# A hybrid mixer layer: the small attention products of two chunks merged into one step, and some weight and key steps moved

## The chip, the cores and the metric

The kernel runs on one core of a Trainium2 chip. The metric is device time in microseconds (us) for one execution. TensorE is called PE in the profile, VectorE DVE, ScalarE ACT, GpSimd POOL, and SyncE, which issues DMAs, SP.

## The reference, cut to what matters

1024 prompt tokens and 64 sample tokens (8 sequences of 8) pass one layer with 1024 channels. One input projection feeds two mixers and their gates:

```
u, gp, q, k, v, gg, fa = split(x @ w_in)          # 512, 512, 256, 256, 512, 512, 16 columns
# pooling: per group of 128 channels a trailing mean over 2/4/8/16 tokens, minus the token, then a 128x128 map
pool_out = (mean_window(u) - u) @ w_map * scale
# gated linear attention, 4 heads, key width 64, value width 128, decays from fa
S_t = diag(a_t) S_{t-1} + k_t^T v_t ;  o_t = q_t S_t ;  o = o * rsqrt(mean(o*o) + eps) * norm_g
mix = concat(pool_out * silu(gp), o * silu(gg))
out = LayerNorm(alpha * x + mix @ w_out) * ln_g + ln_b
```

All of it is in 32-bit floats. The outputs are the tokens' results, the last pooling inputs, and the attention states of prompt and samples.

## The kernel before

**Split products.** Each large product takes its operands as a high and a low part of reduced precision (`split`: ScalarE copies the high part, VectorE or GpSimd subtracts the low one) and runs three matmuls (`mm3`, lines L68 to L70). Prompt attention runs in eight blocks of 128 tokens, c = 0 to 7 (`gla_steps(c)`), the samples are c = 8; the projection runs in three token chunks `CH` of 384, 384 and 320.

**Stages.** First come the value products (`psv`, to 58 us), with decay factors worked out beside them. Then sixteen rows of the projection, i = 0 to 15, each over the three chunks: `group(i, c)` is 24 matmuls into one `psm` tile. The rows are: 0 to 3 keys and queries, 4 to 7 the pooling input u, 8 to 11 the pooling gate, 12 to 15 the attention gate. The out product with `w_out` follows, from 291 us.

**What sets the order.** Small steps are put into a list by `later(delay, step)`. Behind each group, `tick()` runs the steps that have come due, in the order of their due numbers, and counts one slot on. In this text slot 0 is the group (4, 0), at 111.8 us. For a u group, VectorE's pool chain (`chain()`: window sums `ws`, difference `pd`, its split `pdhl`) is issued behind the tick, and its map product `psmap` later. When c is 0, the weights of row i+1 are split there: ScalarE the high part, GpSimd the low one (`hl` in the profile).

**The small steps of block c.** Line numbers are those of the profile before.

- s1, at number 2c: two PE transposes of the keys into the first 256 columns of a tile `pskt` (L712), four score products (L717), with keys and queries 64 deep, into the other half of `pskt` and into `psa`; then ScalarE copies the keys out (`kt`, L719) and VectorE masks the scores (`am`, L723).
- s2, at 2c+1: kt·v, four products of 64 columns of keys into the first half of `psp_` (L753); the inter products of state and queries, 64 deep (L761), and the intra products with `am` (L763), both into the second half of `psp_` and into `pso`; then the new state `S` by VectorE from `psp_` (L776, L777), squares by ScalarE (`sq`, L799) and their split `sqhl`.
- s3, at 2c+3: sums of squares (`psms`, L808); ScalarE loads a function table, takes Ln and Exp (L810 to L812); VectorE scales the block's output (`vm`, L818).

So an even slot 2c holds s1 of block c, an odd slot 2c+1 holds s3 of block c−1 and s2 of block c.

**The end of the projection.** Behind group (15, 1), `transition()` splits the first mix tile (`mx`) and the second slice of `w_out` (`split_w(17)`); behind group (15, 2) come its gate (silu on ScalarE, three products on VectorE, L401), the third slice, and the loads and splits of the other slices (`split_wo`). `sample_state_prep`, issued in the second round of the out loop, has GpSimd mask the samples' keys (L574) and decay their states. A `safe` variant of everything is built beside the fast one; it does not run with these inputs.

Of the kernel before, what the change touches and what calls it, by code (L numbers as in the profile page):

```python
# [15 lines left out]
D = 1024  # L16
# [23 lines left out]
class Body:  # L40
# [54 lines left out]
    def emit(self):  # L95
# [109 lines left out]

        def split_w(i):
            t = hlp.tile([128, 2, 8, 128] if i < 16 else [128, 2, 1024], F32, tag="hl", name="hl")
            self.split(t[:, 0], t[:, 1], raws.pop(("w", i)), on_lo=nc.gpsimd if i < 16 else None)
            wt[i] = t


# [111 lines left out]
        for t in range(3):  # L323
# [2 lines left out]
            (0, 1, 2): [("s", 2, 0), ("w", 1)],  # L326
            (1, 0, 0): [("lr",)],
            (1, 0, 1): [("s", 2, 4)],
            (2, 1, 0): [("sw", 0), ("w", 2)],
        }  # L330
        def low_rank_weight():

# [36 lines left out]
        def group(i, c):  # L369
            chain = None  # L370
            kind, m = order[i]
            o, n = CH[c]
            ps = psp.tile([128, 512], F32, tag="p", name="psm")
            for k in range(8):
                self.mm3(ps[:, :n], wt[i][:, 0, k], wt[i][:, 1, k], xt_hi[c][:, k], xt_lo[c][:, k], k == 0, k == 7)
            src = ps[:, :n]
            if kind == "k":
                if safe:
                    nc.vector.tensor_copy(self.K[:, m, o:o + n], src)
                else:  # L380
                    nc.vector.tensor_tensor(self.K[:, m, o:o + n], src, EK[:, m, o:o + n], op=ALU.mult)
            elif kind == "q":
                if safe:
                    nc.vector.tensor_scalar(self.Q[:, m, o:o + n], src, 0.125, None, op0=ALU.mult)
                else:
                    nc.vector.scalar_tensor_tensor(self.Q[:, m, o:o + n], src, 0.125, EQ[:, m, o:o + n],
                                                   op0=ALU.mult, op1=ALU.mult)
            elif kind == "u":
                chain = self.pool_steps(m, c, src)
            elif kind == "gp":  # L390
                sg = self.sgp.tile([128, 384], F32, tag="sg", name="sg")
                nc.scalar.activation(sg[:, :n], src, AF.Silu)
                pm = self.pmix[:, m, o:o + n]
                nc.vector.tensor_tensor(pm, pm, sg[:, :n], op=ALU.mult)
            else:
                sg = self.sgp.tile([128, 384], F32, tag="sg", name="sg")
                nc.scalar.activation(sg[:, :n], src, AF.Silu)  # L397
                for t in range(3 * c, 3 * c + 3):
                    _, to, tn = tiles[t]
                    pg = self.v[t][:, m, :tn]  # L400
                    nc.vector.scalar_tensor_tensor(pg, sg[:, to:to + tn], self.norm[:, m:m + 1], pg,  # L401
                                                   op0=ALU.mult, op1=ALU.mult)
            self.tick()
            if chain is not None:
                chain()
            if c == 0:
                split_w(i + 1)
                load_w(i + 3)
            if c == 1 and i == 15:
                self.transition()  # L410
# [13 lines left out]
        self.S = None  # L424
        for c in range(9):
            steps = self.gla_steps(c)
            at = [2 * c, 2 * c + 1, 2 * c + 3] if c < 8 else AT8
            for w, step in zip(at, steps):
                self.later(w, step)

# [2 lines left out]
        def load_wo(k):  # L433
            if k < 6:
                t = lnp.tile([128, D], F32, tag="hh", bufs=3, name="wr")
            else:
                t = rawp.tile([128, D], F32, tag="raw", name="wr")
            nc.sync.dma_start(t, io["w_out"][k])
            wraw[k] = t

# [21 lines left out]
        def transition():  # L462
            split_mix(0)
            split_w(17)

        self.transition = transition

        for i in range(4, 16):
# [13 lines left out]
            if i == 14:  # L482
                for k in (3, 4, 5):
                    load_wo(k)
        split_w(18)
        load_wo(6)
        for k in range(3):
            wo[k] = wt[16 + k]
        split_wo(3)
# [52 lines left out]

        split_wo(4)
        split_wo(5)
        load_wo(7)
        split_wo(6)
        split_wo(7)
        nc.scalar.preload_act_table_set(EXP_LN)
        for j, t in enumerate(OUT_ORDER):
            if j + 1 < 9:  # L550
                split_mix(OUT_ORDER[j + 1])
            out_tile(t)
            if j + 2 < 9:
                load_res(OUT_ORDER[j + 2])
            if j == 1:
                self.sample_state_prep()
            if j == 6:
                for q, pp in enumerate(self.sample_state_mm(0)):
                    self.sample_state_out(0, q, pp)()
# [5 lines left out]
            self.close(name)  # L565


    def sample_state_prep(self):
        nc = self.nc
        t = self.xp.tile([128, 2, 2048], F32, tag="xc2", name="s1")  # L570
        self.s1 = t[:, 0].rearrange("k (p b v) -> k p b v", p=2, b=NB)
        self.km = t[:NS, 1].rearrange("k (b c) -> k b c", b=NB)
        nc.sync.dma_start(self.s1, self.io["s0"])
        nc.gpsimd.tensor_tensor(self.km, self.kt8.unsqueeze(1).broadcast_to([NS, NB, 256]),  # L574
                                self.bmask.unsqueeze(2).broadcast_to([NS, NB, 256]), op=ALU.mult)
        for p in range(2):
            nc.gpsimd.tensor_tensor(self.s1[:, p], self.s1[:, p],
                                    self.dec[:, p, 8:16].unsqueeze(2).broadcast_to([128, NB, 128]), op=ALU.mult)

    def sample_state_mm(self, p, old=False):  # L580

# [92 lines left out]
    def gla_steps(self, c):  # L674
# [23 lines left out]
                st["kd"] = kd  # L698

        def s1():  # L700
            Kst, Qi = K, Q
            am = gl.tile([128, 4, 128], F32, tag="am", bufs=1, name="am")
            st["am"] = am
            if self.safe:
                Kst, Qi = self.safe_scores(c, am, t0, n, sample)
# [4 lines left out]
            pa = [pk[:, 256:], None]  # L710
            for p in range(2):
                nc.tensor.transpose(pk[:n, p * 128:(p + 1) * 128], Kst[:, p], self.ident)  # L712
            if not self.safe:
                pa[1] = g_tile("psa1")
                for h in range(4):
                    r, p = rows[h % 2], h // 2
                    nc.tensor.matmul(pa[h % 2][:n, p * n:(p + 1) * n], K[r, p], Q[r, p], start=True, stop=True)  # L717
            kt = self.kt8 if sample else gl.tile([128, 256], F32, tag="kt", bufs=1, name="kt")
            nc.scalar.activation(kt[:n], pk[:n, :256], AF.Copy)  # L719
            st["kt"] = kt  # L720
            if not self.safe:
                for e in range(2):
                    nc.vector.tensor_tensor(am[:n, two(e), :n], pa[e][:n, :2 * n].rearrange("s (p t) -> s p t", p=2),  # L723
                                            msk[:n, :n].unsqueeze(1).broadcast_to([n, 2, n]), op=ALU.mult)
# [9 lines left out]
        def sample_inter():  # L734
# [9 lines left out]
            st["in"] = gl.tile([128, 512], F32, tag="sin", bufs=1, name="sin")  # L744
            nc.scalar.activation(st["in"], ps, AF.Copy)

        def s2():
            v, am, kt = self.v[c], st["am"], st["kt"]
            if not sample:
                pp = g_tile("psp_")  # L750
                for h in range(4):
                    p = h // 2
                    nc.tensor.matmul(pp[rows[h % 2], p * 128:(p + 1) * 128], kt[:, h * 64:(h + 1) * 64], v[:, h],  # L753
                                     start=True, stop=True)

                po = [pp[:, 256:], g_tile("pso1")]
                dst = [po[h % 2][:, h // 2 * 128:h // 2 * 128 + 128] for h in range(4)]
                if c > 0:
                    for h in range(4):
                        p, r = h // 2, rows[h % 2]  # L760
                        nc.tensor.matmul(dst[h], self.S[r, p], st["Qi"][r, p], start=p == 0, stop=False)  # L761
                for h in range(4):
                    nc.tensor.matmul(dst[h], v[:, h], am[:, h], start=c == 0, stop=c == 0 or h >= 2)  # L763
                sn = self.S if self.safe and c > 0 else gl.tile([128, 2, 128], F32, tag="S", bufs=1 if self.safe else 2, name="S")
                ppv = pp[:, :256].rearrange("k (p v) -> k p v", p=2)
                db = self.dec[:, :, c:c + 1].broadcast_to([128, 2, 128])
                if c == 0:
                    if self.safe:
                        nc.vector.tensor_copy(sn, ppv)
                    else:  # L770
                        nc.vector.tensor_tensor(sn, ppv, db, op=ALU.mult)
                elif self.safe:
                    nc.vector.tensor_tensor(sn, self.S, db, op=ALU.mult)
                    nc.vector.tensor_tensor(sn, sn, ppv, op=ALU.add)
                else:
                    nc.vector.tensor_tensor(sn, ppv, self.S, op=ALU.add)  # L776
                    nc.vector.tensor_tensor(sn, sn, db, op=ALU.mult)  # L777
                self.S = sn
                if c == 7:
                    nc.gpsimd.dma_start(self.io["o_sp"], sn)  # L780
# [47 lines left out]

        if sample:
            return [s0, s0k, s1, sample_inter, s2, s3]  # L830
        return [s1, s2, s3]

# [173 lines left out]
```

## Time and profile before

| | us |
|---|---|
| runs | 406.49, 403.39, 405.49 (median 405.49) |
| profiled execution | 405.02 |
| its span | 403.2 |
| mean granted TensorE clock | 0.991 |
| TensorE busy | 389.0 (96%) |
| VectorE, ScalarE, GpSimd busy | 216.8, 145.1, 56.8 |

The timeline has a row for each instruction: start, duration, engine, line, operation, output and inputs, and in brackets the idle time ahead of it with what ended that. On TensorE a row's duration is longer than its distance to the next row, since the array is pipelined; distances of starts are what a product costs. A table of windows lists for each engine its busy time, then the granted clock, the share of DMA and GB/s. A row of waits gives the total, the number and the longest.

### The profile page before, as it was taken

The page shows a single profiled execution, that of the slowest core. Times are in us where ns is not written, and L with a number is a line of the kernel's source. Part 1 is how long each engine was busy: PE and PEld are TensorE (multiplying, and loading weights), DVE is VectorE, ACT ScalarE, POOL GpSimd, SP SyncE. Part 2 cuts the span into 40 slices and gives each one's busy share as a digit, 9 for nine tenths or more (in the row PEclk, how much of TensorE's full clock was granted, in tenths as well). Part 3 has the DMA queues.
Part 4 walks back from the last instruction along what each step waited for, and adds up shares of the span by engine and source line. Part 5 has one row for each costly group of instructions (what it writes and reads, how often), then busy time and mean ns, then how long its engine had stood idle before and what let it go on. Part 6 is the DMA issues. An engine that isn't in the chain of part 4 may idle for free.

```text
span 403.2 us, 6076 instructions
## 1 busy us (share of the span) xinstructions
PE 389.0 (96%) x2477; PEld 360.0 (89%) x2477; DVE 216.8 (54%) x411; ACT 145.1 (36%) x256; POOL 56.8 (14%) x50
## 2 busy tenths in 40 slices
PE   8999999999999999999999999999979999999991
PEld 7999989999999999999899999999958888888780
DVE  3775354412154877788633311212597658555782
ACT  5544354410034465456657124312463111001201
POOL 1000022240020202031102220232020023000000
PEclk9999999999999999999999999999989999999998
DMA  8960011040010101040102110166230353332413
GB/s 257 384 232 1 2 53 54 0 158 0 2 52 2 53 2 54 0 153 5 54 8 59 54 52 0 54 238 232 80 106 0 104 211 104 104 106 78 156 28 112
DMA packets 11557, 34.29 MB, mean 85 GB/s; under 512 B 1777, under 2 KB 3233, under 8 KB 11265
## 3 DMA queue, kind: packets, MB, share of 16 engines
q1 hardware_dynamic: 10672, 31.71, 23.1%
q0 software_dynamic: 416, 1.46, 0.9%
q10 hardware_dynamic: 432, 0.66, 0.5%
q8 instruction: 21, 0.34, 0.3%
q14 instruction: 16, 0.12, 0.1%
HBM read 27.91 MB, written 5.91 MB: 84 GB/s over the span
## 4 chain that ended last, share of the span: by engine, by line
PE 83%; DVE 8%; ACT 4%; issue 2%; POOL 1%; ACTq 0%; DVEq 0%; POOLq 0%
PE psm L68 14%; PE psm L69 13%; PE psm L70 13%; PE pso L69 7%; PE pso L70 7%; PE pso L68 7%; PE psv L68 4%; PE psv L69 4%; PE psv L70 4%; DVE ws L650 3%; DVE pdhl L64 1%; PE psw L189 1%; PE pso L75 1%; PE pso L78 1%; PE pskt L717 1%
## 5 line engine op out<-in xcount | busy, mean ns | idle before, releaser
L68 PE MATMUL psm<-xc,hl 128*128 128x384 f32 (+1 forms) x384 | 126.1, 328 | 0.9 <-DVE fats L246 0.9
L70 PE MATMUL psm<-xc,hl 128*128 128x384 f32 (+1 forms) x384 | 125.2, 326 | 0.0
L69 PE MATMUL psm<-xc,hl 128*128 128x384 f32 (+1 forms) x384 | 125.1, 326 | 0.0
L68 PEld LDWEIGHTS psm<-xc,hl 128*128 128x128 f32 x384 | 72.1, 188 | 1.8 <-ACT vs L240 1.1
L69 PEld LDWEIGHTS psm<-xc,hl 128*128 128x128 f32 x384 | 72.1, 188 | 0.0
L70 PEld LDWEIGHTS psm<-xc,hl 128*128 128x128 f32 x384 | 72.1, 188 | 0.0
L64 POOL TENSOR_TENSOR hl<-raw,hl 128x1024 fp32r<-128x1024 f32 x16 | 39.0, 2440 | 187.8 <-ACT hl L61 187.8
L68 PE MATMUL psv<-wv,xc 128*128 128x264 f32 x128 | 36.8, 288 | 0.0
L69 PE MATMUL psv<-wv,xc 128*128 128x264 f32 x128 | 36.5, 285 | 0.0
L70 PE MATMUL psv<-wv,xc 128*128 128x264 f32 x128 | 36.5, 285 | 0.0
L68 PE MATMUL pso<-wo,mx 128*128 128x512 f32 (+1 forms) x85 | 32.2, 379 | 0.0
L69 PE MATMUL pso<-wo,mx 128*128 128x512 f32 (+1 forms) x85 | 32.2, 379 | 0.0
L70 PE MATMUL pso<-wo,mx 128*128 128x512 f32 (+1 forms) x85 | 32.1, 377 | 0.0
L401 DVE SCALAR_TENSOR_TENSOR vm<-sg,vecs,vm 128x128 f32<-128x128 f32 (+1 forms) x36 | 13.7, 436 | 31.7 <-ACT sg L397 31.7
L527 ACT ACTIVATE mv<-mv,eps 128x1 f32<-128x1 f32 (+1 forms) x9 | 2.7, 295 | 72.1 <-DVE mv L526 72.1
L520 DVE SCALAR_TENSOR_TENSOR hh<-xr,pso 128x512 f32<-128x512 f32 (+2 forms) x19 | 12.4, 653 | 23.4 <-PE pso L70 23.3
L69 PEld LDWEIGHTS psv<-wv,xc 128*128 128x128 f32 x128 | 24.4, 191 | 0.1
L68 PEld LDWEIGHTS psv<-wv,xc 128*128 128x128 f32 x128 | 24.4, 191 | 0.1
L70 PEld LDWEIGHTS psv<-wv,xc 128*128 128x128 f32 x128 | 24.2, 189 | 0.0
L636 ACT ACTIVATE ue<-psm 128x384 f32<-128x384 f32 (+1 forms) x12 | 5.5, 456 | 50.4 <-PE psm L70 40.8
L69 PE MATMUL pso<-hl,mx 128*128 128x512 f32 (+1 forms) x51 | 19.9, 389 | 2.6 <-DVE hl L64 2.6
L61 ACT ACTIVATE hl<-raw 128x1024 fp32r<-128x1024 f32 x19 | 19.9, 1051 | 5.4 <-PE psm L70 5.4
(240 smaller groups left out, 622.3 us busy)
## 6 DMA issues: line engine op xcount, KB each, us to landing
raw<-wm_dram SPq DMA_DIRECT2D x16, 512.0 KB, 3.5
xr<-x_dram SPq DMA_DIRECT2D x8, 512.0 KB, 4.3
o_y_dram<-hh SPq DMA_DIRECT2D x7, 512.0 KB, 2.9
wr<-w_out_dram SPq DMA_DIRECT2D x5, 512.0 KB, 4.6
s<-s_dram SPq DMA_DIRECT2D x2, 1024.0 KB, 7.0
hl<-xt_dram SPq DMA_DIRECT2D x2, 768.0 KB, 6.7
raw<-w_out_dram SPq DMA_DIRECT2D x3, 512.0 KB, 3.6
hl<-xt_dram SPq DMA_DIRECT2D x2, 640.0 KB, 5.7
```

The lines of the kernel that those rows point to most:

```text
L61: self.nc.scalar.activation(hi.bitcast(FR), raw, AF.Copy)
L64: (on_lo or self.nc.vector).tensor_tensor(lo.bitcast(FR), raw, hi, op=ALU.subtract)
L68: nc.tensor.matmul(ps, ahi.bitcast(FR), bhi.bitcast(FR), start=first, stop=False)
L69: nc.tensor.matmul(ps, ahi.bitcast(FR), blo.bitcast(FR), start=False, stop=False)
L70: nc.tensor.matmul(ps, alo.bitcast(FR), bhi.bitcast(FR), start=False, stop=last)
L75: one = lambda st, sp: nc.tensor.matmul(ps, both.bitcast(FR), bhi.bitcast(FR), start=st, stop=sp)
L78: nc.tensor.matmul(ps[:64], both[:, :64].bitcast(FR), blo.bitcast(FR), start=False, stop=False)
L189: nc.tensor.matmul(psw, warm[:, :128].bitcast(FR), warm.bitcast(FR), start=True, stop=True)
L401: nc.vector.scalar_tensor_tensor(pg, sg[:, to:to + tn], self.norm[:, m:m + 1], pg, op0=ALU.mult, op1=ALU.mult)
L520: nc.vector.scalar_tensor_tensor(hh[:n, s], x[:n, s], ALPHA if n == 128 else 1.0, ps[h][:n, :wd], op0=ALU.mult, op1=ALU.add)
L636: nc.scalar.activation(ue[:, HIST:HIST + np_], src[:, :np_], AF.Copy)
L650: nc.vector.tensor_tensor(nxt[:, lo:width], cur[:, lo:width], cur[:, lo - d:width - d], op=ALU.add)
```

## The change

1. For blocks 0 to 7, s1 is cut into s1a (transposes, kt copy) and s1b (scores, am), and s2 into s2p (kt·v and the new state S) and s2 (inter, intra, squares). They are due at 2c−0.9, 2c−0.7, 2c+1.2, 2c+1.4; s3 stays at 2c+3. An even slot then runs transposes of block c+1, kt·v of block c, scores of c+1, inter and intra of c; an odd slot has s3 alone. `kt` and `am` have two buffers. The state S is issued right behind kt·v.
2. The first weights' split moves from the value product (2, 1, 0) to (2, 0, 0), with its low part on VectorE.
3. The third `w_out` slice is split in `transition()`; the VectorE gate of group (15, 2) is put off until behind the second mix tile's split; slices 6 and 7 are loaded together into a buffer of their own.
4. The samples' keys and states are prepared by ScalarE, in three parts over rounds 1 to 3 of the out loop.

```diff
-            self.split(t[:, 0], t[:, 1], raws.pop(("w", i)), on_lo=nc.gpsimd if i < 16 else None)
+            self.split(t[:, 0], t[:, 1], raws.pop(("w", i)), on_lo=nc.gpsimd if 0 < i < 16 else None)
...
-            (2, 1, 0): [("sw", 0), ("w", 2)],
+            (2, 0, 0): [("sw", 0), ("w", 2)],
...
+                if (i, c) != (15, 2):
+                    gate()
+                else:
+                    self.last_gate = gate
...
-            at = [2 * c, 2 * c + 1, 2 * c + 3] if c < 8 else AT8
+            at = AT8
+            if c < 8:
+                at = [2 * c, 2 * c + 1, 2 * c + 3] if safe else [2 * c - .9, 2 * c - .7, 2 * c + 1.2, 2 * c + 1.4, 2 * c + 3]
...
-                t = rawp.tile([128, D], F32, tag="raw", name="wr")
+                if k == 6:
+                    wo["wr"] = xp.tile([128, 2, D], F32, tag="xc2", name="wr2")
+                t = wo["wr"][:, k - 6]
...
             split_w(17)
+            split_w(18)
...
-        split_w(18)
         load_wo(6)
+        load_wo(7)
...
+            if j == 0:
+                self.last_gate()
             out_tile(t)
...
-            if j == 1:
-                self.sample_state_prep()
+            if j in (1, 2, 3):
+                self.sample_state_prep(j - 1)
...
+        for b in range(NB):
+            if part == 0:
+                nc.scalar.activation(self.km[:, b], self.kt8, AF.Copy, scale=self.bmask[:, b:b + 1])
+            else:
+                s = self.s1[:, part - 1, b]
+                nc.scalar.activation(s, s, AF.Copy, scale=self.dec[:, part - 1, 8 + b:9 + b])
...
+        def s2p():
+            v, kt = self.v[c], st["kt"]
+            pp = st["pp"] = g_tile("psp_")
+            for h in range(4):
+                p = h // 2
+                nc.tensor.matmul(pp[rows[h % 2], p * 128:(p + 1) * 128], kt[:, h * 64:(h + 1) * 64], v[:, h],
+                                 start=True, stop=True)
+            old = st["S"] = self.S
+            sn = old if self.safe and c > 0 else gl.tile([128, 2, 128], F32, tag="S", bufs=1 if self.safe else 2, name="S")
+            st["sn"] = sn
+            if not self.safe:
+                decay()
...
-        return [s1, s2, s3]
+        return [s1, s2, s3] if self.safe else [s1a, s1b, s2p, s2, s3]
```

**TensorE, blocks 1 and 2 around slots 4 and 5.** Names with numbers are tiles of one kind; a bracket lists what the instruction waits for. Before, slot 4 (the first five rows) and slot 5:

```order
L712 MATMUL pskt<-ident,K 128x128 [waits Activation_49]
L712 MATMUL pskt<-ident,K 128x128
L717 MATMUL pskt<-Q,K 128x128
L717 MATMUL psa_1484<-Q,K 128x128 [waits DVE_49]
...
L68 MATMUL psmap<-pdhl,wmap 128x320 [waits DVE_49]
...
L808 MATMUL psms<-sqhl,ones 128x512 [waits Activation_49]
...
L753 MATMUL psp__1549<-vm,kt 64x128 [waits DVE_49]
L753 MATMUL psp__1549<-vm,kt 64x128 x3
L761 MATMUL psp__1549<-Q,S 128x128
L761 MATMUL pso_1554<-Q,S 128x128 [waits Activation_49]
...
L763 MATMUL psp__1549<-am,vm 128x128
L763 MATMUL pso_1554<-am,vm 128x128 [waits DVE_49]
```

In the change, slot 4:

```order
L734 MATMUL pskt<-ident,K 128x128 [waits PE_49]
L734 MATMUL pskt<-ident,K 128x128
L776 MATMUL psp__1463<-vm,kt 64x128 [waits Activation_49]
L776 MATMUL psp__1463<-vm,kt 64x128 x3
L745 MATMUL pskt<-Q,K 128x128 [waits Activation_49]
L745 MATMUL psa_1471<-Q,K 128x128
...
L814 MATMUL psp__1463<-Q,S 128x128 [waits DVE_49]
L814 MATMUL pso_1478<-Q,S 128x128
...
L816 MATMUL psp__1463<-am,vm 128x128
L816 MATMUL pso_1478<-am,vm 128x128
...
L68 MATMUL psmap<-pdhl,wmap 128x320 [waits PE_49]
```

The four kinds of products stand in one tick. Two waits are new in it: the first score product (L745) waits for ScalarE's copy of the keys from the same `pskt`, and the first inter product (L814) waits for VectorE's read of the same `psp_`, the state S.

**VectorE, the odd slot 3 and what follows.** `vm` is the output of block 0, `ws` to `pdhl` the pool chain of the group (5, 0), `S` the new state. Before:

```order
L818 TENSOR_TENSOR vm<-psp__1288,rs 128x2x128 [waits Activation_49]
L818 TENSOR_TENSOR vm<-pso_1293,rs 128x2x128
L776 TENSOR_TENSOR S<-psp__1409,S 128x256 [waits PE_49]
L777 TENSOR_TENSOR S<-S,dec 128x256 [waits DVE_49]
L64 TENSOR_TENSOR sqhl<-sq,sqhl 128x512 [waits Activation_49]
L650 TENSOR_TENSOR ws<-ue 128x398 [waits Pool_49]
L650 TENSOR_TENSOR ws<-ws 128x396 [waits DVE_49]
L653 TENSOR_TENSOR ws<-ws,corr 128x16 [waits DVE_49]
L656 SCALAR_TENSOR_TENSOR pd<-ws,ue 128x384 [waits DVE_49]
```

In the change:

```order
L856 TENSOR_TENSOR vm<-psp__1333,rs 128x2x128 [waits Activation_49]
L856 TENSOR_TENSOR vm<-pso_1347,rs 128x2x128
L668 TENSOR_TENSOR ws<-ue 128x398 [waits Pool_49]
L668 TENSOR_TENSOR ws<-ws 128x396 [waits DVE_49]
L671 TENSOR_TENSOR ws<-ws,corr 128x16 [waits DVE_49]
L674 SCALAR_TENSOR_TENSOR pd<-ws,ue 128x384 [waits DVE_49]
L63 CAST pdhl<-pd 128x384 [waits DVE_49,PE_49]
L64 TENSOR_TENSOR pdhl<-pd,pdhl 128x384 [waits DVE_49]
L652 COPY ue<-ue 128x15
L797 TENSOR_TENSOR S<-psp__1463,S 128x256 [waits PE_49]
L798 TENSOR_TENSOR S<-S,dec 128x256 [waits DVE_49]
```

The state S of block 1 has moved from ahead of the slot's pool chain to behind it.

**ScalarE, the end of the projection.** `sg` are silus of the gate groups, `mx` the mix tile, `hl` slices of `w_out`. Before:

```order
L397 ACTIVATE sg<-psm 128x384 [waits DVE_49,PE_49,Activation_49]
L458 ACTIVATE mx<-pmix 128x4x128 [waits DMASW0_49]
L458 ACTIVATE mx<-vm 128x4x128 [waits DVE_49]
L61 ACTIVATE hl<-raw 128x1024 [waits DMAHW3_49,Pool_49]
L397 ACTIVATE sg<-psm 128x320 [waits DVE_49,PE_49,Activation_49]
L61 ACTIVATE hl<-raw 128x1024 [waits DMAHW7_49,Pool_49]
```

In the change:

```order
L397 ACTIVATE sg<-psm 128x384 [waits DVE_49,PE_49,Activation_49]
L471 ACTIVATE mx<-pmix 128x4x128 [waits DMASW0_49]
L471 ACTIVATE mx<-vm 128x4x128 [waits DVE_49]
L61 ACTIVATE hl<-raw 128x1024 [waits DMAHW3_49,Pool_49]
L61 ACTIVATE hl<-raw 128x1024 [waits DMAHW7_49,PE_49,Pool_49]
L397 ACTIVATE sg<-psm 128x320 [waits DVE_49,Activation_49]
```

The third slice now stands ahead of the last silu, and has a wait for TensorE more.

More of the change, by code (lines that the diff above doesn't have):

```diff
@@ L397, in group, with gate @@
                 nc.scalar.activation(sg[:, :n], src, AF.Silu)
[L398 to L402, printed above, removed]
+                def gate():
+                    for t in range(3 * c, 3 * c + 3):
+                        _, to, tn = tiles[t]
+                        pg = self.v[t][:, m, :tn]
+                        nc.vector.scalar_tensor_tensor(pg, sg[:, to:to + tn], self.norm[:, m:m + 1], pg,
+                                                       op0=ALU.mult, op1=ALU.mult)
+                if (i, c) != (15, 2):
+                    gate()
+                else:
+                    self.last_gate = gate
             self.tick()
@@ L544, in emit @@
         split_wo(5)
-        load_wo(7)
         split_wo(6)
@@ L565, in emit, with sample_state_prep @@
             self.close(name)
-    def sample_state_prep(self):
+    def sample_state_prep(self, part):
         nc = self.nc
[L570 to L578, printed above, removed]
+        if part == 0:
+            t = self.xp.tile([128, 2, 2048], F32, tag="xc2", name="s1")
+            self.s1 = t[:, 0].rearrange("k (p b v) -> k p b v", p=2, b=NB)
+            self.km = t[:NS, 1].rearrange("k (b c) -> k b c", b=NB)
+            nc.sync.dma_start(self.s1, self.io["s0"])
+        for b in range(NB):
+            if part == 0:
+                nc.scalar.activation(self.km[:, b], self.kt8, AF.Copy, scale=self.bmask[:, b:b + 1])
+            else:
+                s = self.s1[:, part - 1, b]
+                nc.scalar.activation(s, s, AF.Copy, scale=self.dec[:, part - 1, 8 + b:9 + b])
     def sample_state_mm(self, p, old=False):
@@ L700, in s1, with s1a @@
         def s1():
+            s1a()
+            s1b()
+        def s1a():
             Kst, Qi = K, Q
-            am = gl.tile([128, 4, 128], F32, tag="am", bufs=1, name="am")
+            am = gl.tile([128, 4, 128], F32, tag="am", bufs=1 if self.safe else 2, name="am")
             st["am"] = am
@@ L712, in s1, with s1b @@
                 nc.tensor.transpose(pk[:n, p * 128:(p + 1) * 128], Kst[:, p], self.ident)
+            kt = self.kt8 if sample else gl.tile([128, 256], F32, tag="kt", bufs=1 if self.safe else 2, name="kt")
+            nc.scalar.activation(kt[:n], pk[:n, :256], AF.Copy)
+            st["kt"], st["pa"] = kt, pa
+        def s1b():
+            am, pa, Qi = st["am"], st["pa"], st["Qi"]
             if not self.safe:
@@ L717, in s1 @@
                     nc.tensor.matmul(pa[h % 2][:n, p * n:(p + 1) * n], K[r, p], Q[r, p], start=True, stop=True)
[L718 to L721, printed above, removed]
                 for e in range(2):
@@ L745, in sample_inter, with decay @@
             nc.scalar.activation(st["in"], ps, AF.Copy)
+        def s2p():
[10 more added lines that the diff above has]
+                decay()
+        def decay():
+            sn, old = st["sn"], st["S"]
+            ppv = st["pp"][:, :256].rearrange("k (p v) -> k p v", p=2)
+            db = self.dec[:, :, c:c + 1].broadcast_to([128, 2, 128])
+            if c == 0:
+                if self.safe:
+                    nc.vector.tensor_copy(sn, ppv)
+                else:
+                    nc.vector.tensor_tensor(sn, ppv, db, op=ALU.mult)
+            elif self.safe:
+                nc.vector.tensor_tensor(sn, old, db, op=ALU.mult)
+                nc.vector.tensor_tensor(sn, sn, ppv, op=ALU.add)
+            else:
+                nc.vector.tensor_tensor(sn, ppv, old, op=ALU.add)
+                nc.vector.tensor_tensor(sn, sn, db, op=ALU.mult)
+            self.S = sn
+            if c == 7:
+                nc.gpsimd.dma_start(self.io["o_sp"], sn)
         def s2():
@@ L749, in s2 @@
             if not sample:
[L750 to L756, printed above, removed]
+                if self.safe:
+                    s2p()
+                po = [st["pp"][:, 256:], g_tile("pso1")]
                 dst = [po[h % 2][:, h // 2 * 128:h // 2 * 128 + 128] for h in range(4)]
@@ L760, in s2 @@
                         p, r = h // 2, rows[h % 2]
-                        nc.tensor.matmul(dst[h], self.S[r, p], st["Qi"][r, p], start=p == 0, stop=False)
+                        nc.tensor.matmul(dst[h], st["S"][r, p], st["Qi"][r, p], start=p == 0, stop=False)
                 for h in range(4):
                     nc.tensor.matmul(dst[h], v[:, h], am[:, h], start=c == 0, stop=c == 0 or h >= 2)
[L764 to L780, printed above, removed]
+                if self.safe:
+                    decay()
             else:
```

## The prediction

> **What bounds the kernel now.** I read the page's first part, then TensorE's waits, then the timeline of each engine around the steps that move.
>
> ```profile
> PE 389.0 (96%) x2477; PEld 360.0 (89%) x2477; DVE 216.8 (54%) x411; ACT 145.1 (36%) x256; POOL 56.8 (14%) x50
> PE pso L69 <- DVE hl L64: 2.6, 1, 2.6
> PE psm L68 <- DVE fats L246: 0.9, 1, 0.9
> PE pso L761 <- DVE am L723: 0.5, 1, 0.5
> ```
>
> TensorE is busy for 96% of the span; its waits (total, times, longest) behind the warm-up are three, 4.0 us in all. So any gain must come out of those, out of time lost between its instructions, or out of a lower clock; and any new wait of TensorE is paid in full. I call the end of a slot's 24-matmul group G. This is what follows in an odd slot and then in an even one:
>
> ```profile
> 127.99 0.63 PE L808 MATMUL psms<-sqhl,ones 128*128 128x512 f32 x2
> 128.54 0.66 PE L753 MATMUL psp__1409<-vm,kt 128*64 128x128 f32 x8
> 129.13 0.37 PE L761 MATMUL psp__1409<-Q,S 64*128 64x128 f32 x1
> 129.78 0.49 PE L763 MATMUL psp__1409<-am,vm 128*128 128x128 f32 x2
> 130.69 0.42 PE L68 MATMUL psmap<-pdhl,wmap 128*128 128x384 f32 x1
> 131.31 0.33 PE L68 MATMUL psm<-xc,hl 128*128 128x384 f32 x1
> ...
> 135.47 0.38 PE L712 MATMUL pskt<-ident,K 128*128 128x128 f32 x2
> 135.78 0.37 PE L717 MATMUL pskt<-Q,K 64*128 64x128 f32 x1
> ...
> 135.99 0.27 PE L717 MATMUL pskt<-Q,K 64*128 64x128 f32 x1
> ...
> 136.11 0.27 PE L717 MATMUL pskt<-Q,K 64*128 64x128 f32 x1
> ...
> 136.43 0.41 PE L68 MATMUL psmap<-pdhl,wmap 128*128 128x320 f32 x1
> ```
>
> By differences of starts: sums of squares 0.55 (G to kt·v), kt·v 0.59, Sᵀq (inter) 0.65, am·v (intra) 0.91, pool map 0.62, a group 4.16, two transposes 0.31, scores 0.65. Once under way, the scores' passes (four products in two passes each, run as four pairs) follow 0.11 apart (135.99 to 136.11), so four pairs should take 0.43. The 0.22 beyond it lies at their ends, where the shape of the array changes, and inter shows the same. Shared between the two ends that is 0.11 for a change; charged to one of them it is 0.22. I take 0.15.
>
> **What the merge removes.** In an odd and an even tick together there were five changes of shape (scores in and out; kt·v in, inter in, intra in); in the merged even tick there are three (kt·v, scores with inter, intra). Over the chunks 13 go: 13 × 0.15 = **−2.0** (−1.4 to −2.8). Up to 0.9 of the changes that stay or go may fall inside waits; I count that below as −0.9, with 0 as its other bound.
>
> **What the merge adds: two waits inside one tick.** By the instruction order, inter (first write into psp_) now waits for the S step of the same tick, which reads the same psp_ tile on VectorE, and scores wait for ScalarE's kt copy out of pskt. Before, S came behind all of TensorE's writes. That these are treated as one resource is visible in the trace: two reads of one psp_ tile in disjoint columns do not overlap.
>
> ```profile
> ACT sq L799 <- DVE S L776: 9.8, 7, 2.6
> 132.05 0.41 DVE L776 TENSOR_TENSOR S<-psp__1409,S 128x256 f32<-128x256 f32 x1
> 132.56 0.38 ACT L799 ACTIVATE sq<-psp__1409 128x256 f32<-128x256 f32 x1 [1.21 <-DVE S L776]
> ```
>
> The copy of squares waited for S seven times and began 0.10 after S ended. The Trainium skill's "PSUM — Partial Sum Buffer", section "PSUM bank collisions raise a hardware error", says that two engines must not be on one bank at once, reads with reads included, so that software must order them; it is the rule that speaks against this change, and by the 0.10 above the trace agrees. Without that order the sum below would lose its largest term.
>
> When can S run? On VectorE it stands behind the odd slot's whole queue: vm (waits for ScalarE's Ln and Exp), then the pool chain of that slot.
>
> ```profile
> 128.70 1.28 ACT L810 ACT_TABLE_LOAD   x1
> 131.38 0.42 DVE L818 TENSOR_TENSOR vm<-psp__1288,rs 128x256 f32<-128x256 f32 x1 [4.82 <-ACT rs L812]
> 134.52 0.57 DVE L650 TENSOR_TENSOR ws<-ue 128x398 f32<-128x398 f32 x1
> 135.73 2.24 DVE L653 TENSOR_TENSOR ws<-ws,corr 128x16 f32<-128x16 f32 x1
> 139.54 0.17 DVE L634 COPY ue<-ue 128x15 f32<-128x15 f32 x1
> 135.38 2.56 POOL L64 TENSOR_TENSOR hl<-raw,hl 128x1024 fp32r<-128x1024 f32 x1 [11.78 <-ACT hl L61]
> ```
>
> With G = 127.99, vm starts at G+3.39 because the table load, Ln and Exp stand behind each other, none of which the change shortens; two vm of 0.34 bring the pool chain to G+4.07 (S and sqhl, which stood between, leave). The chain of this slot lasts 139.54 − 134.52 = 5.02 = L: about 3.0 of work, and 2.0 because its tiny correction (2.24) runs beside GpSimd's split (2.56). S then starts at G+4.07+L+0.1 and inter 0.45 later, at G+4.6+L. TensorE's next group ends at G+0.43+0.62+4.16 = G+5.2 now (the odd tick holds only sums of squares and pool map), 4.6 or so after a 320 group. From there it has 0.31 transposes, 0.59 kt·v, 0.54 scores, 1.44 of own work, until it wants inter. The **stall is L − 2.0** where the even slot's group has 384 columns and **L − 1.4** where it has 320. The other odd chains:
>
> ```profile
> 147.09 0.63 DVE L650 TENSOR_TENSOR ws<-ue 128x454 f32<-128x454 f32 x1
> 149.85 0.42 DVE L723 TENSOR_TENSOR am<-pskt,mask 128x256 f32<-128x256 f32 x1
> ...
> 160.31 0.57 DVE L650 TENSOR_TENSOR ws<-ue 128x398 f32<-128x398 f32 x1
> 163.76 0.17 DVE L634 COPY ue<-ue 128x15 f32<-128x15 f32 x1
> ...
> 172.78 0.57 DVE L650 TENSOR_TENSOR ws<-ue 128x398 f32<-128x398 f32 x1
> 179.00 0.17 DVE L634 COPY ue<-ue 128x15 f32<-128x15 f32 x1
> ...
> 187.00 0.62 DVE L650 TENSOR_TENSOR ws<-ue 128x454 f32<-128x454 f32 x1
> 190.66 2.56 DVE L64 TENSOR_TENSOR pdhl<-pd,pdhl 128x320 fp32r<-128x320 f32 x1
> ...
> 213.61 1.07 DVE L394 TENSOR_TENSOR pmix<-pmix,sg 128x384 f32<-128x384 f32 x1 [1.79 <-ACT sg L392]
> ```
>
> L by rows: slot 5 149.85 − 147.09 = 2.76; slot 7 3.45; slot 9 6.22 (again beside GpSimd); slot 11 187.00 to 190.66 plus a low part that should be 0.5, not the 2.56 of a collision which the shift moves away, 4.1. So the stalls are: slot 4, 3.0; slot 6, 0.7; slot 8, 2.1; slot 10, 4.2; slot 12, 2.1 and a pool gate of 0.4 that stands ahead of S, 2.5. Slots 14 and 16 have no chain; the gate products on VectorE stand ahead of S there (1.07 in the last row, waiting for a silu): estimates 0.5 and 2.5. The kt wait counts only where nothing later does: the copy begins 0.66 or so after G behind ue, lasts 0.39, and TensorE wants it at G+0.31 in slots 0 and 18 (0.8 each) and at G+0.9 in slot 2 (0.3). Sum 0.8+0.3+3.0+0.7+2.1+4.2+2.5+0.5+2.5+0.8 = **+17.4**. Without any collision with GpSimd it is 12.8, the lower bound. The one wait of before in a merged place, the 0.5 for am (the L761 row above), goes: **−0.5**.
>
> **The clock after a long wait.** The trace has one wait of such a size:
>
> ```profile
> 293.81 0.39 PE L70 MATMUL pso<-hl,mx 128*128 128x512 f32 x1
> 294.04 0.39 PE L68 MATMUL pso<-hl,mx 128*128 128x512 f32 x1
> 297.02 0.79 PE L69 MATMUL pso<-hl,mx 128*128 128x512 f32 x1 [2.60 <-DVE hl L64]
> 297.00:300.50 3.50, 3.48 (x9) 2.75 (x10) 3.50 (x4) 0.04 (x1) 0.00 (x0) 0.54 0.50 154
> 291.53 3.69 POOL L574 TENSOR_TENSOR s<-kt,bmask 64x2048 f32<-64x2048 f32 x1 [15.60 <-PE psm L70]
> 292.82 3.88 ACT L61 ACTIVATE wo<-wr 128x1024 fp32r<-128x1024 f32 x4
> 292.01 3.83 DVE L401 SCALAR_TENSOR_TENSOR vm<-sg,vecs,vm 128x128 f32<-128x128 f32 x3 [0.24 <-ACT sg L397]
> ```
>
> After 2.60 us of idle TensorE the granted clock was 0.54 for 3.5 us: 3.5 × 0.46 = 1.6 us more. After the 0.9 and the 0.5 it stayed up. Five of my stalls are 2.1 to 4.2 long; I charge three of them, 3 × 1.6 = **+4.8**, between 0 and 5 × 1.6 = 8.0. The Trainium skill's "TensorE: Matmul & The Clock Gate", section "Why this matters for your kernels", asks for no idle gap above about 3 us. By that rule the wait of 2.60 should have been free, which the 0.54 contradicts here.
>
> **The step into the output product.** The same rows show its cause: GpSimd's key product (3.69) beside the last gates of VectorE (3.83 for three), and behind them the low part of w_out's split. The change gives the keys to ScalarE later, moves the last gate behind that split and the split ahead of the last silu. L69 then follows at 294.04 + 0.23: 297.02 − 294.27 = 2.75, and with it the 1.6 of half clock: **−4.35**. What is late next is w_out's fourth to eighth splits, each 1.0 on ScalarE (3.88 for four), against 1.4 of TensorE per slice of w_out (six matmuls at the 0.23 from 293.81 to 294.04); they keep ahead. If one came late, the 2.75 is the most that would come back. The 24 small ScalarE steps of the keys and states lie in the output product, where that engine mostly waits; I cost them at nothing. Without that cover the price is bounded by the nearest ScalarE rows, of 0.38 and more: 24 × 0.4 = 10.
>
> **First weights.** The 0.9 wait at the key groups ends when VectorE has brought the low-rank inputs of the gate (fats), behind work that ran beside GpSimd's split of the first weights. That split now stands three value products earlier and on VectorE, so the wait goes: **−0.9**, with 0 as the other bound; GpSimd's collisions above show how a VectorE step stretches beside it.
>
> **Sum**, against the profiled execution's 405.02 (span 403.2, the median of the runs is 405.49): 405.02 − 2.0 + 17.4 − 0.5 + 4.8 − 4.35 − 0.9 − 0.9 = **418.6**. Bounds: 12.8 of stalls with no half clock gives 409.2; 8.0 of half clock and no hidden changes of shape gives 422.7.
>
> **Rivals.**
> - *S comes in time* (faster). Were the odd chains' ends at most G+6.1 (L of 2.0 or less), no long stall is left: kt waits of 1.9 alone give 405.02 − 2.0 − 0.5 + 1.9 − 4.35 − 0.9 = 399.2. For it: VectorE is busy for 54% only. Against it: every L above is over 2.0, and vm cannot start before Exp. Chance 0.10.
> - *No collisions, clock stays up*: 409.2 or a little above, since GpSimd's splits follow ScalarE's and those move. Half of that relief, or stalls shortened in another way, ends near no change. 0.26 together, 0.09 of it within 1%.
> - *Only idle above 3 us lowers the clock*: only slot 10 would pay 1.6, 418.6 − 3.2 = 415.4; the 2.60 speaks against it. The Trainium skill's page named above gives that bound. 0.08.
> - *Every long stall pays half clock*: 418.6 + 3.2 = 421.8. 0.12.
> - *The changes of shape are not saved* because the waits part the products anyway: the sum without −2.0, 420.6. 0.06.
> - *The forecast*, 418.6 within 2: 0.38.
>
> Faster by over 1% (about what a measurement can tell from no change; below 401.4) 0.10, within 1% 0.09, slower by over 1% (above 409.5) 0.81. The range 406 to 424 leaves out the faster rival and some of the no-change cases.
>
> **What would show it.** In the changed profile's waits of TensorE: psp_ (inter) behind VectorE's S, some seven to nine times, longest near 4, 15 or so in all; pskt behind the kt copy, near 0.8 twice; no pso L69 wait of 2.6; no fats wait of 0.9. Granted clock below 0.8 behind the longest stalls. Scores and inter should stand 0.43 each without a change between them. I am wrong if inter starts 1.5 after its group's end in most even slots, that is, if VectorE's S does not stand behind the chain in time, or if ScalarE's new steps hold up the mix splits of the output product.

## The result, and the profile after

The changed kernel takes 421.6 us (415.96 to 423.03), the one before 405.5: 1.037 times as long, 95% interval 1.027 to 1.046. The forecast was 418.6. The profiled execution took 415.96 (span 414.0) at a mean granted clock of 0.985, the timed ones about 421.5 at 0.97; why these differ is taken up with the clock below.

TensorE's waits in the changed kernel (total, times, longest):

```profile
PE psp__1885 L814 <- DVE S L797: 3.8, 1, 3.8
PE psp__1463 L814 <- DVE S L797: 2.6, 1, 2.6
PE psp__2030 L814 <- DVE S L797: 2.2, 1, 2.2
PE psp__2251 L814 <- DVE S L797: 2.1, 1, 2.1
PE psp__1742 L814 <- DVE S L797: 1.9, 1, 1.9
PE pskt L745 <- ACT kt L736: 1.9, 4, 0.6
PE psp__1598 L814 <- DVE S L797: 0.5, 1, 0.5
```

The two waits that the instruction order announced are there, 13.1 for S and 1.9 for the key copy; the waits for `hl`, `fats` and `am` are gone. By stages: up to the first matmul of the first key group 1.4 less, of it 0.9 the `fats` wait, and 0.5 in the first value products (taken up with the clock below); from the end of slot 0's group to the out product 196.2 against 179.5, **16.7 more**; the out product 96.0 against 100.4, **4.4 less**. How one wait comes about, in the timelines of slots 3 and 4:

```profile
127.26 0.62 PE L846 MATMUL psms<-sqhl,ones 128*128 128x512 f32 x2
130.65 0.42 DVE L856 TENSOR_TENSOR vm<-psp__1333,rs 128x256 f32<-128x256 f32 x1 [3.96 <-ACT rs L850]
131.32 0.56 DVE L668 TENSOR_TENSOR ws<-ue 128x398 f32<-128x398 f32 x1
132.52 2.21 DVE L671 TENSOR_TENSOR ws<-ws,corr 128x16 f32<-128x16 f32 x1
132.11 2.59 POOL L64 TENSOR_TENSOR hl<-raw,hl 128x1024 fp32r<-128x1024 f32 x1 [11.04 <-ACT hl L61]
132.43 0.38 PE L734 MATMUL pskt<-ident,K 128*128 128x128 f32 x2
136.38 0.42 DVE L797 TENSOR_TENSOR S<-psp__1463,S 128x256 f32<-128x256 f32 x1
136.85 0.37 PE L814 MATMUL psp__1463<-Q,S 64*128 64x128 f32 x1 [2.64 <-DVE S L797]
```

The group of slot 3 ends at 127.26. `vm` starts 3.39 later, the pool chain 4.06 later; it lasts 5.06, its correction of 16 columns taking 2.21 beside GpSimd's split. S follows at 136.38, and inter 0.05 after S ends. TensorE came to the end of its next group at 132.43, and had nothing to do from the end of the scores on. The wait is one that the program carries (L814 `[waits DVE_49]` in the order above); no run shows what the chip would do without it.

### The profile page after: what moved, and what is told of

Read it like the earlier page. It is cut to its first block, busy times and chain, and to the rows that moved or that the text cites. A ratio compares the mean times of both kernels' runs of the same rounds, so it can differ in the third digit from the quotient of the medians.

```text
span 414.0 us, 6105 instructions
## 1 busy us (share of the span) xinstructions
PE 388.2 (94%) x2477; PEld 361.2 (87%) x2477; DVE 208.9 (50%) x412; ACT 151.6 (37%) x280; POOL 44.6 (11%) x46
## 4 chain that ended last, share of the span: by engine, by line
PE 83%; ACT 7%; DVE 6%; issue 1%; POOL 0%; ACTq 0%; DVEq 0%; POOLq 0%
PE psm L68 13%; PE psm L70 13%; PE psm L69 13%; PE pso L69 7%; PE pso L68 7%; PE pso L70 7%; PE psv L68 4%; PE psv L69 4%; PE psv L70 4%; DVE ws L668 3%; ACT L848 2%; ACT rs L849 1%; PE psw L189 1%; PE pso L816 1%; PE pso L75 1%
## 5 line engine op out<-in xcount | busy, mean ns | idle before, releaser
L64 POOL TENSOR_TENSOR hl<-raw,hl 128x1024 fp32r<-128x1024 f32 x15 | 36.4, 2431 | 213.1 <-ACT hl L61 213.1
L403 DVE SCALAR_TENSOR_TENSOR vm<-sg,vecs,vm 128x128 f32<-128x128 f32 (+1 forms) x36 | 10.7, 352 | 31.5 <-ACT sg L397 31.5
L394 DVE TENSOR_TENSOR pmix<-pmix,sg 128x384 f32<-128x384 f32 (+1 forms) x12 | 6.9, 573 | 28.6 <-ACT sg L392 28.6
```

Source lines behind the costliest of these rows:

```text
L64: (on_lo or self.nc.vector).tensor_tensor(lo.bitcast(FR), raw, hi, op=ALU.subtract)
```

## The experiments

**The merge undone.** The small products are issued in the old order, with S behind intra and the key copy behind the scores; the three other edits stay.

```diff
-                at = [2 * c, 2 * c + 1, 2 * c + 3] if safe else [2 * c - .9, 2 * c - .7, 2 * c + 1.2, 2 * c + 1.4, 2 * c + 3]
+                at = [2 * c, 2 * c + 1, 2 * c + 3] if safe else [2 * c, 2 * c, 2 * c + 1, 2 * c + 1, 2 * c + 3]
...
             st["sn"] = sn
-            if not self.safe:
-                decay()
...
-                if self.safe:
-                    decay()
+                decay()
```

> The small products stand in the old order (transposes, scores, then the key copy; kt·v, inter, intra and then S one slot later); the other edits stay. If the merge alone makes the change slow, what is left are the gains of the other edits: 4.4 at the step into the output product (as the trace of the changed kernel shows, 100.4 against 96.0 from its first to its last big matmul) and 1.0 at the first weights, so 405.5 - 5.4 = 400.1, with no wait of TensorE over 0.6. If one of the other edits costs something that the waits hide, it stays above 402.

399.6 us, 0.9891 of the kernel before (0.985 to 0.9931). From slot 0 to the out product it takes 179.45, as before, and has one wait:

```profile
PE pso L815 <- DVE am L750: 0.4, 1, 0.4
```

So the merge alone is what makes the change slow, and the other edits bring about 1%.

**The merge alone**, without the three other edits.

```diff
-            self.split(t[:, 0], t[:, 1], raws.pop(("w", i)), on_lo=nc.gpsimd if 0 < i < 16 else None)
+            self.split(t[:, 0], t[:, 1], raws.pop(("w", i)), on_lo=nc.gpsimd if i < 16 else None)
...
-            (2, 0, 0): [("sw", 0), ("w", 2)],
+            (2, 1, 0): [("sw", 0), ("w", 2)],
...
-            split_w(18)
...
-            if j == 0:
-                self.last_gate()
...
-            if j in (1, 2, 3):
-                self.sample_state_prep(j - 1)
+            if j == 1:
+                self.sample_state_prep()
```

> The kernel before with the merge alone, without the three other edits. If the parts add up, it stands as far above the changed kernel as the kernel with the merge undone stands below the one before: 421.6 + 5.0 = 426.6, with the waits of both, 13.1 for S, 1.9 for the key copy, 2.6 at the third slice and 0.9 at the first weights. If the merge's waits take up some of the others (GpSimd's splits fall elsewhere), it stays under 424.

426.4 us, 1.0515 (1.0433 to 1.0597); its waits are those of both kernels. The waits add up to 0.1, the time within its spread of 423.3 to 430.3.

**S behind intra.** Merged order, but `decay()` moved from the end of s2p to the end of s2, behind the squares and their split.

```diff
             st["sn"] = sn
-            if not self.safe:
-                decay()
...
             st["hl"] = hl
+            if not sample and not self.safe:
+                decay()
```

> The merged order stays, but VectorE's new state S is issued behind the intra products, the squares and their split, so inter no longer stands behind S's read of psp_. If the wait for S is what costs, all six waits for S (13.1 us) and the low clock behind them go, the four waits for the key copy (1.9) stay: 400.1 - 0.5 + 1.9 = 401.5 less up to 2.0 for the changes of shape, so 399.5 to 401.5. If merging in itself holds TensorE up (the late VectorE queue through am or sqhl, say), waits of another name take the place and it stays over 408.

398.8 us, 0.9873 (0.9834 to 0.9913). All that TensorE waits for is the key copy:

```profile
PE pskt L745 <- ACT kt L736: 1.9, 4, 0.6
137.51 0.42 DVE L795 TENSOR_TENSOR S<-psp__1463,S 128x256 f32<-128x256 f32 x1
```

S itself runs 1.1 later than in the changed kernel (137.51 against 136.38), and nothing waits for it. It is in slot 6 that its value is wanted.

**A tile of its own for kt·v.** S stays at its early place.

```diff
-                po = [st["pp"][:, 256:], g_tile("pso1")]
+                po = [st["pp"][:, 256:] if self.safe else g_tile("pso0"), g_tile("pso1")]
```

> The merged order stays and S stays at its early place, but kt·v has a tile of its own and inter and intra go into two others, so S and inter no longer share one. If the shared tile makes the wait, the waits for S go although S runs as late as before: 399.5 to 402, with a small wait possible because there is one tile more in the ring of six. If TensorE waits for S as data or through the order of issue, it stays near 421 with about 13 us of waits.

398.4 us, 0.9871 (0.9828 to 0.9913). No wait for S is left, and no other than the key copy's 1.9 comes with the additional tile. Timelines of slot 4:

```profile
135.98 0.41 DVE L797 TENSOR_TENSOR S<-psp__1464,S 128x256 f32<-128x256 f32 x1
133.64 0.61 PE L814 MATMUL pso<-Q,S 64*128 64x128 f32 x8
```

S is as late as in the changed kernel (its chain ends at the same distance behind the group), yet inter starts 2.3 ahead of it. So neither the merge nor the late S costs time. The waits for S come from inter and S sharing one PSUM tile while VectorE's S stands behind the pool chain.

**A longer chain.** The changed kernel with the first window sum of each odd chain made twice more.

```diff
+                if s == 0 and (3 * g + c) % 2 and not self.safe:
+                    for _ in range(2):
+                        nc.vector.tensor_tensor(nxt[:, lo:width], ue[:, lo:width], ue[:, lo - d:width - d], op=ALU.add)
```

> The changed kernel with two more VectorE instructions in the pool chain of each odd slot (the first window sum made twice more, the same values), 0.6 each. If S waits for that queue, each of the stalls in slots 4, 6, 8, 10 and 12 grows by 1.2, the waits for S in all from 13.1 to about 19, the time by 6 and by what a lower clock adds: 422 to 430. If the stalls come from elsewhere, the 1.2 are hidden and the waits stay near 13.

425.7 us in one execution, 9.8 above the changed kernel's profiled one.

```profile
PE psp__1895 L817 <- DVE S L800: 5.0, 1, 5.0
PE psp__1467 L817 <- DVE S L800: 3.8, 1, 3.8
PE psp__2042 L817 <- DVE S L800: 3.6, 1, 3.6
PE psp__1750 L817 <- DVE S L800: 3.1, 1, 3.1
PE psp__2263 L817 <- DVE S L800: 2.1, 1, 2.1
PE psp__1604 L817 <- DVE S L800: 1.8, 1, 1.8
```

The waits in slots 4, 6, 8, 10 and 12 are 1.2 to 1.4 longer each; the one of slot 16 (2.1), which has no chain ahead of it, is not. What is added to the chain is paid in full: 6.3 in waits. The other 3.5 goes with the clock, which fell behind four of the waits here (those of slots 4, 8, 10 and 12) and behind one in the changed kernel.

**S late and the products reordered.** As with S behind intra; besides, inter stands ahead of the scores, and in slots 0 and 18 the scores ahead of the transposes.

```diff
-                at = [2 * c, 2 * c + 1, 2 * c + 3] if safe else [2 * c - .9, 2 * c - .7, 2 * c + 1.2, 2 * c + 1.4, 2 * c + 3]
+                at = [2 * c, 2 * c + 1, 2 * c + 3] if safe else [2 * c - .9, 2 * c - .7, 2 * c + 1.2, 2 * c + 1.25, 2 * c + 1.4, 2 * c + 3]
...
+            if not self.safe and c in (0, 8):
+                scores()
             for p in range(2):
                 nc.tensor.transpose(pk[:n, p * 128:(p + 1) * 128], Kst[:, p], self.ident)
...
-        return [s1, s2, s3] if self.safe else [s1a, s1b, s2p, s2, s3]
+        return [s1, s2, s3] if self.safe else [s1a, s1b, s2p, s2i, s2, s3]
```

> S behind intra as in the kernel with S late, and two more changes of order: inter ahead of the scores, and in slots 0 and 18 the scores ahead of the transposes, so that the key copy has time. Expected are no waits for S and none for the key copy: 400.1 - 0.5 less 0.5 to 2.0 for the changes of shape = 397.6 to 399.1. If the shapes save nothing, 399.6; if scores and inter run no closer than before, the same.

396.1 us, 0.9809 (0.9769 to 0.9849), the fastest of all. One wait is left, and the timeline of slot 4 shows inter, scores and intra close together:

```profile
PE pskt L747 <- ACT kt L739: 0.2, 1, 0.2
132.58 0.37 PE L815 MATMUL psp__1463<-Q,S 64*128 64x128 f32 x1
...
133.13 0.27 PE L747 MATMUL pskt<-Q,K 64*128 64x128 f32 x1
...
133.68 0.49 PE L825 MATMUL psp__1463<-am,vm 128*128 128x128 f32 x2
```

Eight products 64 deep take 1.10 (132.58 to 133.68), where scores and inter apart took 0.65 each. From slot 0 to the out product it is 176.2 against the 179.45 of the merge undone: 3.25 less, of it 0.2 by waits (0.4 against 0.2), so **3.05 for 13 changes of shape, 0.23 each**, if nothing else in the new order gains (the trace of the merge undone has 46 changes in this stretch, this one 33). With the 1.9 of key waits still in, S behind intra gains 0.5 there, so 2.0 for the shapes. Most of what it falls short by are pauses for the key copy that are too short for the table of waits: in slots 4 to 12 its scores begin 0.71 to 0.77 behind the start of kt·v, not 0.59, 0.75 in all.

**Keys by ScalarE alone; the moved split and gate alone.** Each is the kernel before with one of the edits that bear on the step into the out product, the fourth and the third of the change; their diffs stand there.

> The kernel before with one edit: the samples' keys and states are prepared by ScalarE in three parts, not by GpSimd. If GpSimd's key product alone stretched the last gates, they take 0.9 again, the third slice's low part ends at about 294.1 and the wait of 2.6 goes with its low clock: 405.5 - 4.4 = 401.1. If the order of split and gate matters as well, a wait of 1 or more is left: 402.5 to 404.

> The kernel before with one other edit: the third slice split ahead of the last silu, the last gate put off, slices 6 and 7 loaded together. GpSimd's key product still starts behind the last keys at 291.5 and runs 3.7; the third slice's low part then runs beside it instead of the gates, 1.2 stretched to about 2.5, ending near 295.2: a wait of 1 to 1.5 at the third slice, 405.5 - 1.3 = 404.2, or 402.6 if the clock stays up behind it. If the order alone is the cure, no wait is left: 401.1.

They take 400.9 (0.9903, 0.9865 to 0.9941) and 400.4 (0.9893, 0.9855 to 0.993): each removes the whole wait. For the second the expectation was wrong. VectorE's last gates and low part in the first, then VectorE's low part and GpSimd's key product in the second:

```profile
292.56 0.81 DVE L401 SCALAR_TENSOR_TENSOR vm<-sg,vecs,vm 128x128 f32<-128x128 f32 x3 [0.24 <-ACT sg L397]
293.50 1.22 DVE L64 TENSOR_TENSOR hl<-raw,hl 128x1024 fp32r<-128x1024 f32 x1
...
292.58 1.22 DVE L64 TENSOR_TENSOR hl<-raw,hl 128x1024 fp32r<-128x1024 f32 x1 [0.87 <-ACT hl L61]
299.75 3.99 POOL L585 TENSOR_TENSOR s<-kt,bmask 64x2048 f32<-64x2048 f32 x1 [23.88 <-DVE wo L64]
```

In the first the three gates take 0.81 with GpSimd idle, where they took 3.83 beside the key product. In the second the key product still exists, but begins 8 us later: its buffer is the one that slices 6 and 7 now take, and it waits until their low parts are made (`<-DVE wo`). I had read the edit's order and not its buffer. What the order alone would do, with the buffer as it was, isn't shown.

**The clock: the same kernel again, and shifted.** The last four runs change nothing but the number of warm-up matmuls at the start (9 as they are, 13, 17, 21).

```diff
-        for _ in range(9):
+        for _ in range(13):
             nc.tensor.matmul(psw, warm[:, :128].bitcast(FR), warm.bitcast(FR), start=True, stop=True)
```

> The changed kernel once more, for the clock: its profiled execution took 415.96 with a mean granted clock of 0.985, its other runs about 421.5 at 0.97. If the difference is the number of long waits behind which the clock drops, the waits are again 13.1 for S and 1.9 for the key copy, and a slower execution shows 0.5 or so behind more of the five long waits, 1.5 to 3 us each. If the waits themselves differ between executions, their sum is 4 or more above 15.0.

> The changed kernel with four more of the warm-up matmuls at its start, which shift everything behind by 0.9 us. The waits should be the same, 15.0. If the length of a wait alone decides whether the clock drops, it drops behind the 3.8 of slot 10 alone again, and the time is 415.9 + 0.9 = 416.8. If the place of the wait against the clock's own periods decides, other waits of 1.9 to 2.6 show 0.5 to 0.7 behind them, or slot 10's doesn't: 414 to 423.

> As with four more, with eight: shifted by 1.7 us. By the length alone 417.6, with the drop at slot 10 only; by the place against the clock's periods another set of drops than in the unshifted kernel or the one shifted by 0.9.

> As before, with twelve: shifted by 2.6 us. By the length alone 418.5, with the drop at slot 10 only; by the place against the clock's periods a set of drops of its own.

415.91, 420.25, 423.08 and 424.46 in one execution each, where the shift alone would give 415.9, 416.8, 417.6 and 418.5. The waits agree to 0.1 in all four (3.8, 2.6, 2.2, 2.1, 1.9, 0.5 for S). Windows of 2.5 us behind the waits of 2.6, 3.8 and 2.1, first of the changed kernel, then of the one shifted by eight; behind the engines' busy times stands the granted clock:

```profile
136.80:139.30 2.50, 2.45 (x22) 2.33 (x23) 1.09 (x3) 0.75 (x3) 0.09 (x1) 1.00 0.28 111
181.40:183.90 2.50, 2.49 (x14) 2.27 (x15) 1.08 (x3) 0.00 (x0) 0.04 (x1) 0.50 0.76 315
224.70:227.20 2.50, 2.46 (x22) 2.35 (x23) 0.43 (x1) 0.77 (x3) 1.25 (x2) 1.00 0.79 239
...
138.40:140.90 2.50, 2.46 (x14) 2.24 (x15) 1.09 (x3) 0.00 (x0) 0.07 (x1) 0.50 0.24 97
186.10:188.60 2.50, 2.49 (x14) 2.27 (x15) 1.08 (x3) 0.00 (x0) 0.05 (x1) 0.51 0.73 305
230.10:232.60 2.50, 2.45 (x15) 2.23 (x16) 0.43 (x1) 0.00 (x0) 1.25 (x2) 0.59 0.73 252
```

The same wait of 2.6, or of 2.1, is followed by 1.00 in one execution and 0.50 or 0.59 in another. In the changed kernel only slot 10 pays, in the kernel with four more matmuls three waits do, and in the other two all five. So the length alone doesn't decide between 1.9 and 2.7 us; behind every wait of 3.1 and more that was seen, in any kernel, the clock fell.

What decides is in the same traces. Their record of the granted clock has the half clock, ahead of the kernel's last microseconds, only in stretches of 3.41 us or of twice that: in the kernel shifted by eight from 138.38, 169.10, 186.16, 203.23 and 230.54, which lie 9, 5, 5 and 8 times 3.413 apart; in the changed kernel one double stretch, 179.92 to 186.75. So time can be cut into periods of 3.41 us that end where the stretches begin. In the next rows TensorE's busy time is the second number, and the granted clock the third from the end. The first five are the waits of 2.6 and 2.1 in the changed kernel, each cut in two by the end of a period; the others are those of 2.6 and 1.9 in the kernel shifted by eight, mostly or wholly in one period:

```profile
132.14:135.55 3.41, 1.97 (x21) 1.33 (x19) 3.24 (x4) 0.77 (x2) 2.57 (x1) 1.00 0.00 0
135.55:138.97 3.42, 2.12 (x20) 2.00 (x21) 2.30 (x7) 0.45 (x2) 0.29 (x1) 1.00 0.48 156
138.97:142.38 3.41, 3.41 (x25) 3.41 (x25) 2.33 (x5) 1.25 (x3) 0.00 (x0) 1.00 0.00 0
220.88:224.30 3.42, 1.71 (x15) 1.22 (x13) 1.69 (x6) 2.40 (x3) 2.35 (x1) 1.00 0.00 0
224.30:227.71 3.41, 2.98 (x26) 2.86 (x27) 0.81 (x3) 1.28 (x3) 1.25 (x2) 1.00 0.62 192
...
134.96:138.38 3.42, 0.75 (x10) 0.52 (x8) 3.25 (x6) 0.08 (x1) 1.52 (x2) 1.00 0.27 79
138.38:141.79 3.41, 3.35 (x18) 3.13 (x19) 1.09 (x4) 0.46 (x2) 0.09 (x1) 0.50 0.19 77
165.68:169.10 3.42, 1.68 (x17) 1.56 (x18) 2.63 (x8) 0.02 (x1) 0.11 (x1) 1.00 0.02 5
169.10:172.51 3.41, 3.41 (x13) 3.41 (x12) 2.00 (x4) 1.74 (x4) 0.00 (x0) 0.50 0.00 0
```

In the eight traces that have such a drop, between the first value products and the last microseconds, every period at full clock in which TensorE was idle for 1.73 us or more was followed by one at half clock (24 of them), and none in which it was idle for 1.71 or less: the limit is half a period. A second period at half clock followed where 0.8 or more of a wait ran on into the first, as in slot 10 of the changed kernel, and none where it was under 0.3. So a wait's place decides as well as its length. By these periods no single wait under 1.7 us lowers the clock, and every one over 3.41 does. A period at half clock costs 1.7 us (3.41 × 0.5), less by half of what TensorE idles in it. For the three shifted kernels, from the times by the shift alone without the 2.7 of slot 10's drop, that gives 420.5, 423.4 and 424.3.

The periods are not tied to the kernel's start: counted back from the drops, the first one begins 2.4, 2.3, 2.1, 1.8 and 3.4 us behind it in the changed kernel, its repeat and the three shifted ones. What sets that isn't shown. The 0.5 in the first value products fits in: these follow 0.22 apart up to 6.56 in the kernel before and 0.12 apart from 5.88 on in the changed one, and a period counted back this way ends at 6.66 and at 5.84. The timed executions of the unshifted kernel took 5.6 us longer than the profiled one. Five single periods at half clock instead of the one double stretch would make that 415.96 − 2.7 + 8.5 = 421.8; the course of their clock isn't on record.

## Why the prediction was right

- **S behind the pool chain.** Right in mechanism, and the tile of its own shows it. The working gave for slots 4, 6, 8, 10, 12 and 16 stalls of 3.0, 0.7, 2.1, 4.2, 2.5, 2.5; the waits are 2.6, 0.5, 1.9, 3.8, 2.2, 2.1. Each is 0.2 to 0.4 too large. In slots 4 to 12 the step at fault is the 1.44 of own work, not the queue: in slot 4 inter came at 127.26 + 9.59, by the working 4.6 + 5.06 = 9.66, but TensorE was ready for it only at 136.85 − 2.64 = 134.21, 1.78 behind its group (1.73 to 1.79 in slots 4 to 12). The scores began at 133.49, 0.75 behind the start of kt·v instead of 0.59, since they waited for the key copy there too, and lasted 0.72 instead of 0.54. Slot 14's estimated 0.5 did not appear.
- **The key copy**: 1.9 forecast, 1.9 measured. That the sums agree is in part luck: forecast were 0.8, 0.3 and 0.8 in slots 0, 2 and 18, measured 0.64, 0.20 and 0.62 there, and 0.46 in slot 14, where none was forecast.
- **GpSimd's collisions** stayed where they were, in the chains ahead of slots 4 and 10 (2.21 for 16 columns above): the rival without them is out.
- **The changes of shape** (−2.0, and −0.9 hidden in waits). In the changed kernel 16.7 = 15.0 of waits − 0.5 + 2.7 by the clock (half from 179.92 to 186.75, of which TensorE idled until 181.41), which leaves −0.5 for the shapes, not −2.9. Where the waits are gone the saving is 2.0 to 3.05. So the rival that the waits would eat it was mostly right, and the price of a change is 0.23, above the 0.15 taken, where nothing waits.
- **The clock** (+4.8, three drops at 1.6). The price was near, 1.7 for a period at half clock; the count was not. The profiled execution has one drop, of two periods, which cost 2.7. The kernels shifted by eight and twelve have five drops, and the timed executions, at 421.6, fit five as well; that is the rival in which every long stall pays, priced at 421.8. The step that was missing is that a wait's place in the periods counts, so the number of drops changes from execution to execution. The forecast of 418.6 lies between the two kinds of execution for that reason. The rival with idle above 3 us only, 415.4, described the profiled execution and not the others; the Trainium skill's "TensorE: Matmul & The Clock Gate", section "Why this matters for your kernels", which asks for no gap above about 3 us, agrees with the drops that always came from 3.1 on, but not with those behind 1.9 to 2.7.
- **The out product** (−4.35): 4.4. Its reason was half right: the collision is the cause, but either edit alone removes it.
- **First weights** (−0.9): the `fats` wait is gone. It stays, 0.9 long, in the merge alone and in each of the two kernels with one edit, so it is the second edit that removes it.
- **The sum** is closer than its terms. The waits were forecast 2.4 too large (17.4 against 15.0) and the saving by the shapes 2.4 too large (2.9 against 0.5), and these cancel; that is luck. What is left between 418.6 and the 421.6 measured is mostly the clock, 8.5 against 4.8 if its drops were five.
- *S in time*, the faster rival, was priced at 399.2 with key waits only. It is not this kernel, but the one with S behind intra, at 398.8.

## What to carry to other kernels

In this kernel, another engine's instruction that reads a PSUM tile into which a product is still to be written became a wait of TensorE on everything queued ahead of that instruction. Before products are moved together, read the other engine's queue in front of each such reader, and give the reader a tile of its own or issue it behind the last write. Here a tile of its own was one line, and the change went from 3.7% slower to 1.3% faster; with S behind intra instead and the products reordered it was 1.9% faster. A gap in TensorE can cost more than its length: as the clock fell here, a gap of 1.7 to 3.4 us may cost 1.7 more, by its place in the periods, and a longer one always brought a drop. So one profiled execution doesn't show what such a kernel takes.

## What the runs showed of the hardware

- The granted clock was 0.50 in whole periods of 3.41 us. It fell behind a period in which TensorE had idled for more than half (1.73 and more; up to 1.71 it did not fall). So the same wait of 1.9 lowered it in some executions and not in others. A period at half clock costs 1.7.
- Thirteen changes of the array's shape, between products 64 and 128 deep or wide, cost about 0.23 each where nothing waits, and next to nothing where TensorE waits between the products anyway (3.05 and 0.5 saved).
- GpSimd's work beside VectorE's stretched a product of 16 columns from 0.18 (in a slot without such work) to 2.21, and three gates from 0.81 to 3.83.
